# The gates of a gated-DeltaNet mixer as seven half-size products, with the combinations of x written over x

## The chip, the cores and the metric

The kernel runs on one core of a Trainium2 chip. The metric is the time of one execution on the device in microseconds (us); the median of three runs before the change is 1221.23 us (1221.22 to 1221.33). Beside the runs there is one profiled execution, whose trace the hardware profiler took. In what follows TensorE is the matrix engine (PE in the profile, PEld its loading of stationary operands), VectorE is DVE, ScalarE is ACT, GpSimd is POOL and SyncE is SP; a queue marked with a small q issues transfers.

## The reference, cut to what matters

A trunk of two layers over x of 512 tokens by 1024 channels, everything in float32. Layer 0 mixes tokens with gated linear attention (GLA), layer 1 with a gated DeltaNet (GDN); after each mixer comes a gated ConvFFN, and each sublayer ends in a LayerNorm of the scaled residual. The change lies in layer 1's mixer:

```python
def gdn_mixer(x, w_in, conv_w, a_log, dt_bias, norm_w, w_out):
    proj = x @ w_in
    qkv, gate, beta_lin, a_lin = ...            # gate: 512 x 1024
    ...
    o = rms_norm(gdn_chunked(qc, kc, vc, beta, gc), norm_w)
    return (from_head_chunks(o) * jax.nn.silu(gate)) @ w_out

def step(state, inp):                           # of gdn_chunked, over the chunks of tokens
    qk_n, u_n, w_n, qd_n, kd_n, cd_n = inp      # qd = q * exp(bcum)
    v_new = u_n - w_n @ state
    o_n = qd_n @ state + qk_n @ v_new
    state = state * cd_n + kd_n.T @ v_new
```

The gate is a product of x (512 x 1024) with 1024 columns of `w_in`. The kernel takes chunks of 128 tokens, four of them, for its eight heads.

## The kernel before, in words

**Numbers.** Each float32 operand of a large product is kept as a high part and a low part (`xh` and `xl`, `wh` and `wl`) in a type that TensorE takes in one pass, and a product is three matmuls: high with high, high with low, low with high. `split_out` (L715) makes the parts: a cast on ScalarE and a subtraction on VectorE, so both engines work on every weight tile. x itself lies in SBUF as `xh` and `xl`, eight chunks of 128 channels by 512 tokens, and is the operand of every projection of the mixer.

**Weights.** A plan lists all weight tiles in the order of their use. `issue` (L292) loads 128 x 1024 values into one of three buffers `raw` on SyncE's queue and splits them into one of four pairs `wh`, `wl`; `prefetch` runs two or three items ahead of the one taken.

**Order.** The kernel is traced by a planner with a clock of its own. `mm` (L208) adds the cost of each matmul to the clock. Generators (`spawn`) stand for the work beside the large products; each yields the clock time that it wants to let pass and is resumed by `pump` (L184), which is called after every few matmuls of a large product, or by `wait`, which lets the clock run on to the next generator that is due until a flag is set. Flags (`set`, `until`) are times of the planner, and what the chip waits for are the data dependences. A scheduler then places the instructions on the engines' queues by that order, and may take a later instruction where an earlier one isn't ready. Each engine works through its queue in order. Small tiles of 128 x 512 values come from 45 slots in this stage (`SLOTS`, L46).

**GLA's mixer** has its v and its gate as products in the form that the change brings to the other mixer: `plan_gated` (L282) plans the weights, `gated` (L1203) the products, and `x_forms` (L1149) makes the combinations of x, in eight pairs of extra slots. With x and the weight cut in two by two blocks, seven products of half the size in place of eight give the four blocks of the result; `GATED` lists them in order, weight combination and form of x: b21 with a12, b11 with a11, t1 with w1, b22 with v4, t2 with v2, t3 with v3, t4 with a22 (a11 and a12 are the even and odd chunks of tokens 0 to 255, a22 the odd chunks of the rest). The names in the profile are `fold` for their sums in PSUM, `xq` for the combinations and `xfh`, `xfl` for their parts. The weight combinations are made by transfers that add to what lies in SBUF (accumulating transfers, on GpSimd's queue) and by one addition on VectorE (L454).

**GDN's mixer** (`gdn`, L1590) runs the projections of k, v and q (`fm`), and beside them the inverses of small triangular matrices: in `base` on VectorE, with the 128 x 1024 tiles `tt` and `m2`, and in `inverses` on TensorE (`V`, `R`), in ten steps spread over the last projections and the first gate products. Step (half, 3) sets the flag ("rm", 5). Then `gates` (L1279) computes the gate in two halves of 512 columns through `x_tm` and `tm_half` (`tm<-wh,xh` and so on): per half eight channel chunks, four blocks of 128 tokens, three matmuls, each 128 x 128 by 512 columns, with a `pump` after every six. In between runs `chain` (L1888), one for each group of four heads, over four chunks of tokens. A turn of it: the state's product with k (`ks`) gives `yy` on VectorE (L1905); the inverse applied to it (`vn`) is scaled by ScalarE (L1913); k transposed (`kT`) is scaled by ScalarE (L1920); the state's product with q (`qs`) is scaled by VectorE (L1926); `s` updates the state on VectorE (L1936); `o` is added to the outputs on VectorE (L1944), whose squares ScalarE sums (L1946). `finish` (L1964) multiplies gate and output and transposes them (`yT`) for the output projection (`tm<-wh,yh`). After the gate, `unspill` brings the residual back and VectorE rescales it (L987, L988).

Of the kernel before, what the change touches and what calls it, by code (L numbers as in the profile page):

```python
# [8 lines left out]
F32 = mybir.dt.float32  # L9
# [6 lines left out]
P = 128  # L16
# [18 lines left out]
GATED_NEW = {"b21": "b21", "b11": "b11", "t1": "b12", "b22": "b22"}  # L35
GATED_IN = {"b21": "b21", "b11": "b11", "t1": "b11", "b22": "b22", "t2": "b11", "t3": "b22", "t4": "b11"}
GATED_SUM = {"t1": "b22", "b22": "b12", "t2": "b21"}
PREPARE = (4.0, 16.0, 48.0, 68.0)
PREPARE_APART = (2.0, 4.5)
LN_EPS = 1e-5  # L40
# [32 lines left out]
def blk(i, n=P):  # L73
    return slice(i * n, i * n + n)


class Trunk:
# [201 lines left out]
            for i in range(0, group["m"], 2):  # L279
                self.plan.append(("fold", group, name, quarter, i))  # L280

    def plan_gated(self, w, col):  # L282
        group = {"w": w, "col": col}
        for name, _, _ in GATED:
            for i in (0, 2):
                self.plan.append(("gated", group, name, i))
# [151 lines left out]
    def gated_load(self, group, name, i):  # L438


        if name not in GATED_NEW:
            return
        if name == "b11":
            t = self.mp.tile([P, 1024], F32, name=self.uid("gw"), tag="gw", bufs=2)
        else:
            t = self.rp.tile([P, 1024], F32, name=self.uid("raw"), tag="raw")
        self.nc.sync.dma_start(t.rearrange("p (j f) -> p j f", j=2), self.gated_rows(group, GATED_NEW[name], i))
        group[name, i] = t

    def issue_gated(self, group, name, i):  # L450
        nc = self.nc
        t = group[GATED_IN[name], i]
        if name == "t1":
            nc.vector.tensor_add(t, t, group.pop((name, i)))  # L454
            self.vec(1.24)
        self.held += 1
        wh = self.wp.tile([P, 1024], F32R, name=self.uid("wh"), tag="wh")
        wl = self.wp.tile([P, 1024], F32R, name=self.uid("wl"), tag="wl")
        self.split_out(wh, wl, t)
        self.vec(1.24)  # L460
        if name in GATED_SUM:
            nc.gpsimd.dma_start(t.rearrange("p (j f) -> p j f", j=2), self.gated_rows(group, GATED_SUM[name], i),
                                accum_op=ALU.add)
        if name in ("b21", "t3", "t4"):
            del group[GATED_IN[name], i]
        return [(wh[:, blk(j, S)], wl[:, blk(j, S)]) for j in range(2)]
# [101 lines left out]
    def tm_half(self, a, n, tail, done, slots=False, pieces=1):  # L568
# [19 lines left out]
        for tb in range(NTB):  # L588
            m = len(ps[tb])
            for piece in range(m):  # L590
# [5 lines left out]
                    done(tb, ps[tb][0])  # L596
                else:
                    done(tb, ps[tb][piece], piece, blk(piece, S // m))

    def x_tm(self, done):  # L600
        a = lambda c, tb: (self.xh[:, c, blk(tb)], self.xl[:, c, blk(tb)])
        self.tm_half(a, NC, 1, done)

    def out_proj(self, a, n, first, final, pieces=1):

# [543 lines left out]
    def x_forms(self, forms):  # L1149


        nc = self.nc
        pair = lambda t: t.rearrange("p (j i) -> p j i", j=2)

        def part(x, odd, tok, k):
            return x[:, 4 * k + odd:4 * k + odd + 3:2, tok:tok + 256]

        def full(odd, tok):
            ts = [self.slot("xq") for _ in range(2)]
            for k, t in enumerate(ts):  # L1160
                nc.vector.tensor_add(pair(t), *(part(x, odd, tok, k) for x in (self.xh, self.xl)))
            return ts

        def split(name, ts):
            forms[name] = []
            for t in ts:
                h, l = self.slot("xfh", F32R), self.slot("xfl", F32R)
                self.split_out(h, l, t)
                forms[name].append((h, l))
            self.set(("form", name), 2.0)  # L1170

        def both(a, b, op, out):
            for x, y, o in zip(a, b, out):
                nc.vector.tensor_tensor(o, x, y, op)

        for tb in range(NTB):
            yield from self.until(("x", tb))
        a = full(0, 256)
        yield 1.5
        b = full(1, 256)  # L1180
        yield 1.5
        both(a, b, ALU.subtract, b)
        yield 1.5
        split("w1", b)
        yield 2.0
        c = full(0, 0)
        yield 1.5
        both(c, a, ALU.subtract, a)
        yield 1.5
        both(b, c, ALU.subtract, b)  # L1190
        yield 1.5
        c = full(1, 0)
        yield 1.5
        both(b, c, ALU.add, c)
        yield 1.5
        split("v4", c)
        yield 2.0
        split("v2", b)
        b = c = None
        yield 2.0  # L1200
        split("v3", a)

    def gated(self, forms, tag, done, last):  # L1203


# [2 lines left out]
        top, high, right = ([None, None] for _ in range(3))  # L1208

        def operand(form, c, r):  # L1210
            if form in forms:
                cols = slice(c % 2 * 256 + r * P, c % 2 * 256 + r * P + P)
                return tuple(t[:, cols] for t in forms[form][c // 2])
            chunk = 2 * c + (form != "a11")
            tok = r * P + (256 if form == "a22" else 0)
            return self.xh[:, chunk, tok:tok + P], self.xl[:, chunk, tok:tok + P]
# [28 lines left out]
        for name, form, at in GATED:  # L1245
            if form[0] in "vw":
                self.wait(("form", form))
            def terms(i, w, r):
                for j in range(2):
                    begin = name in ("b11", "b21", "t1") and i + j == 0  # L1250
                    self.tm_terms(acc[at][r], *operand(form, i + j, r), *w[j], begin, i + j == 3, True)
                if i:
                    update(name, r)

            if name in ("t1", "t2", "t3"):
                w = [self.weight() for _ in range(2)]
                for r in range(2):
                    for i in (0, 2):
                        if name == "t3" and r and i:
                            self.look = 2  # L1260
                        terms(i, w[i // 2], r)
                        if name != "t3" or not r:
                            self.pump()
                        if r:
                            self.spend()
            else:
                for i in (0, 2):
                    w = self.weight()
                    if name == "t4":
                        self.after = ()  # L1270
                    for r in range(2):
                        terms(i, w, r)
                        self.pump()
                    self.spend()
            if last:
                forms.pop(form, None)
        self.look = LOOKAHEAD

    def gates(self, sg):  # L1279

        for hf in range(2):
            def done(tb, ps, hf=hf):
                t = self.slot("sg")
                self.nc.scalar.activation(t, ps, AF.Silu)
                sg[tb][hf] = t
                self.set(("sg", tb, hf), 2.0)

            self.x_tm(done)


    def gla_plan(self, w_in, w_out):
# [260 lines left out]
    def gdn_plan(self, w_in, w_out):  # L1552
        for hd in range(DH):
            if hd == HEADSTART:
                self.plan_pad([(w_in, 4096, 8, 0), (w_in, 4104, 8, H0)])
            self.plan_fm(w_in, 1024 + hd * P)
        for base in (2048, 0):
            for hd in range(DH):
                self.plan_fm(w_in, base + hd * P)
        for hf in range(2):  # L1560
            for cp in range(NC // 2):
                self.plan_tm(w_in, 2 * cp * P, 2, 3072 + hf * S)
        self.plan_out(w_out, 0, NC, TAIL)

    def gdn_consts(self, conv_w, a_log, dt_bias, norm_w):
# [24 lines left out]
    def gdn(self, li, g, b):  # L1590
# [297 lines left out]
        def chain(g):  # L1888
# [7 lines left out]
            for ck in range(4):  # L1896
# [24 lines left out]
                if ck > 0:  # L1921
                    ps = self.psum("qs")
                    for w, hd in heads:
                        self.mm(ps[:, w], q[hd][:, sl], s[:, w])
                    for w, hd in heads:
                        nc.vector.tensor_scalar_mul(vv[:, w], ps[:, w], eb[:, hd, one])  # L1926
                yield 1.4
                if ck < 3:
                    ps = self.psum("s")
# [31 lines left out]
                                           rr[:, hs4, :], ALU.mult, ALU.mult)  # L1961
            self.set(("r2", g), 2.5)

        def finish(hf):  # L1964
            for tb in range(NTB):
                yield from self.until(("sg", tb, hf))
            yield from self.until(("r2", hf))
            for tb in range(NTB):
                t = sg[tb][hf]
                for hd in range(4 * hf, 4 * hf + 4):  # L1970
                    w = blk(hd % 4)
                    last = nc.vector.scalar_tensor_tensor(t[:, w], v[hf][tb][:, w], r2[:, hd, tb:tb + 1], t[:, w],
                                                          ALU.mult, ALU.mult)
            yield 2.4
            self.split_y(y, hf, sg, self.gdn_nw, after=None if hf else last)

        items = [lambda ps, hd=hd: k_done(ps, hd) for hd in range(DH)]
        items.insert(HEADSTART, ba_done)
# [6 lines left out]
            self.spawn(chain(hg))  # L1985
        self.fm_items(items)
        for hf in range(2):
            self.spawn(finish(hf))
        self.gates(sg)
        self.wait(("r2", 1))  # L1990
        self.unspill(spilled)
        self.mixer_out(y, li, g, b)
# [76 lines left out]
```

## Time and profile before

| | us |
|---|---|
| median of three runs | 1221.23 |
| profiled execution, its own time | 1221.98 |
| its span, first to last instruction | 1220.2 |
| TensorE busy in the span | 1213.6 |
| VectorE busy | 906.1 |
| ScalarE busy | 609.4 |
| GpSimd busy | 160.7 |
| first to last matmul of GDN's gate (`tm<-wh,xh` and its kin, starts) | 724.6 to 813.0 |

The profiled execution took 1.78 us more than its span, and 0.75 us more than the median. Times inside the trace count from the first instruction. A group row gives line, engine, operation, written tile and read tiles, the count after x, then the busy time in us with the mean of one in ns, then the idle time of the engine just ahead of them with what ended it. A matmul row's duration contains its overlap with the next matmul; how fast matmuls follow each other is read from the chain of waits, which gives each piece its own time. A row "... x4" of the timeline gives the time from the first of four instructions to the end of the last.

### The profile page before, as it was taken

What the parts mean: (1) busy time and instruction counts of PE and PEld (TensorE: products, weight loads), DVE (VectorE), ACT (ScalarE), POOL (GpSimd) and SP (SyncE); (2) the same over time, 40 slices, a digit from 0 to 9 for tenths busy, and PEclk for the clock granted to TensorE, in tenths of its full rate; (3) what the DMA queues carried; (4) which work ended last, traced back from release to release, by engine and by line L of the source; (5) the groups of instructions that cost most, each with busy time, mean ns of one, the idle gap of its engine ahead of it and who ended that gap; (6) DMA issues with size and microseconds to landing.
All of it is one profiled execution on the core that took longest, in us unless ns stands there. A gap on an engine that the chain in (4) does not pass through costs nothing.

```text
span 1220.2 us, 17190 instructions
## 1 busy us (share of the span) xinstructions
PE 1213.6 (99%) x6501; PEld 1025.1 (84%) x6501; DVE 906.1 (74%) x1515; ACT 609.4 (50%) x1072; POOL 160.7 (13%) x203
## 2 busy tenths in 40 slices
PE   9999999999999999999999999999999999999998
PEld 8888888988888888889888888988988888888886
DVE  6989787787757675666789965688687757776667
ACT  5666663544434443454678555544644433443440
POOL 3030101601100110001242030200510100020000
PEclk9999999999999999999999999999999999999999
DMA  8384642536743554433444351335444853383311
GB/s 227 113 164 115 141 154 72 189 105 137 190 122 92 124 95 121 123 102 91 125 125 130 87 136 36 101 107 156 135 125 101 170 178 95 104 171 97 108 65 69
DMA packets 176275, 149.41 MB, mean 122 GB/s; under 512 B 16870, under 2 KB 140842, under 8 KB 176192
## 3 DMA queue, kind: packets, MB, share of 16 engines
q1 hardware_dynamic: 162464, 116.28, 32.2%
q0 software_dynamic: 12768, 31.37, 13.0%
q8 instruction: 51, 0.84, 0.3%
q10 hardware_dynamic: 960, 0.66, 0.2%
q14 instruction: 32, 0.26, 0.1%
HBM read 129.92 MB, written 5.78 MB: 111 GB/s over the span
## 4 chain that ended last, share of the span: by engine, by line
PE 97%; DMA 1%; ACT 1%; DVE 1%; SPq 0%; issue 0%; DVEq 0%
PE fm L213 54%; PE fold L213 19%; PE tm L213 15%; PE o L213 2%; PE xT L231 1%; DMA raw<-in_gla_w_in_dram 1%; PE pq L213 1%; PE pg L213 1%; PE vn L213 1%; PE yT L231 1%; PE V L213 0%; PE ds L213 0%; PE qs L213 0%; PE s L213 0%; PE ks L213 0%; DMA raw<-in_gdn_w_in_dram 0%
## 5 line engine op out<-in xcount | busy, mean ns | idle before, releaser
L213 PE MATMUL fm<-xh,wh 128*128 128x512 f32 (+2 forms) x1096 | 400.4, 368 | 0.7 <-ACT xh L716 0.7
L213 PE MATMUL fm<-xl,wh 128*128 128x512 f32 (+2 forms) x1096 | 398.5, 366 | 0.0
L213 PE MATMUL fm<-xh,wl 128*128 128x512 f32 (+1 forms) x1072 | 391.5, 367 | 0.2 <-DVE wl L716 0.2
L716 DVE TENSOR_TENSOR wl<-raw,wh 128x1024 fp32r<-128x1024 f32 (+1 forms) x158 | 195.4, 1239 | 151.7 <-ACT wh L716 151.3
L716 ACT CAST wh<-raw 128x1024 fp32r<-128x1024 f32 (+1 forms) x159 | 164.9, 1039 | 211.2 <-PE fm L213 135.5
L213 PEld LDWEIGHTS fm<-xh,wh 128*128 128x128 f32 (+1 forms) x1096 | 205.4, 188 | 34.1 <-ACT xh L716 0.9
L213 PEld LDWEIGHTS fm<-xl,wh 128*128 128x128 f32 (+1 forms) x1096 | 205.4, 188 | 32.6
L213 PEld LDWEIGHTS fm<-xh,wl 128*128 128x128 f32 x1072 | 201.2, 189 | 33.7 <-DVE wl L716 0.4
L1019 DVE SCALAR_TENSOR_TENSOR conv<-fm,ffn_cw,conv 128x511 f32<-128x511 f32 x112 | 83.5, 745 | 9.6 <-ACT conv L1017 7.9
L213 PE MATMUL fold<-wh,fh 128*128 128x512 f32 x224 | 87.6, 391 | 0.0
L213 PE MATMUL fold<-wh,fl 128*128 128x512 f32 x224 | 87.2, 389 | 0.0
L213 PE MATMUL fold<-wl,fh 128*128 128x512 f32 x224 | 87.1, 389 | 0.0
L716 ACT CAST wh<-b 128x1024 fp32r<-128x1024 f32 x48 | 50.0, 1054 | 74.2 <-PE fold L213 32.5
L716 DVE TENSOR_TENSOR wl<-b,wh 128x1024 fp32r<-128x1024 f32 x48 | 58.1, 1222 | 22.7 <-ACT wh L716 22.5
L412 POOL DMA_DIRECT2D b<-b x24 | 20.8, 902 | 357.2 <-DVE wl L716 306.7
L1037 ACT ACTIVATE conv<-conv 128x512 f32<-128x512 f32 x44 | 27.8, 632 | 63.3 <-DVE conv L1019 63.3
L1585 DVE SCALAR_TENSOR_TENSOR conv<-fm,gdn_cw,conv 128x511 f32<-128x511 f32 (+2 forms) x72 | 54.0, 788 | 5.1 <-ACT conv L1583 4.6
L213 PEld LDWEIGHTS fold<-wh,fh 128*128 128x128 f32 x224 | 42.0, 188 | 9.6 <-DVE h L1108 1.0
L213 PEld LDWEIGHTS fold<-wh,fl 128*128 128x128 f32 x224 | 42.0, 188 | 8.8
L213 PEld LDWEIGHTS fold<-wl,fh 128*128 128x128 f32 x224 | 42.1, 188 | 8.6
L1019 DVE SCALAR_TENSOR_TENSOR form<-fm,ffn_cw,form 128x511 f32<-128x511 f32 x64 | 47.7, 745 | 1.1
L929 POOL TENSOR_TENSOR h<-h,gb 128x512 f32<-128x512 f32 x16 | 24.1, 1525 | 135.5 <-PE xT L231 134.2
(363 smaller groups left out, 2009.1 us busy)
## 6 DMA issues: line engine op xcount, KB each, us to landing
raw<-in_ffn_w_in_dram SPq DMA_DIRECT2D x88, 512.0 KB, 3.9
raw<-in_gdn_w_in_dram SPq DMA_DIRECT2D x32, 512.0 KB, 4.1
b<-in_ffn_w_out_dram SPq DMA_DIRECT2D x24, 512.0 KB, 6.0
b<-b POOLq DMA_DIRECT2D x24, 512.0 KB, 4.8
raw<-in_ffn_w_out_dram SPq DMA_DIRECT2D x20, 512.0 KB, 3.7
raw<-in_gla_w_in_dram SPq DMA_DIRECT2D x18, 512.0 KB, 4.4
gw<-in_gla_w_in_dram POOLq DMA_DIRECT2D x8, 512.0 KB, 7.5
raw<-in_gla_w_out_dram SPq DMA_DIRECT2D x8, 512.0 KB, 3.7
```

The source lines that it names most:

```text
L213: t = self.nc.tensor.matmul(out, a, b, start=start, stop=stop, skip_group_check=joined)
L231: t = self.nc.tensor.transpose(out, a, self.ident[:n, :n])
L412: self.nc.gpsimd.dma_start(out, group[src, i][:, cols], accum_op=ALU.add)
L716: return self.nc.scalar.copy(dst_h, src), self.nc.vector.tensor_sub(dst_l, src, dst_h)
L929: nc.gpsimd.tensor_mul(h[hf], h[hf], gb[hf])
L1019: nc.vector.scalar_tensor_tensor(a[:, d:], ps[:, :S - d], tap(2 - d), a[:, d:], ALU.mult, ALU.add)
L1037: nc.scalar.activation(a, a, AF.Gelu)
L1585: self.conv = nc.vector.scalar_tensor_tensor(a[:, d:], ps[:, :S - d], tap(3 - d), a[:, d:], ALU.mult, ALU.add)
```

## The change

The gate of GDN's mixer becomes a `gated` product: seven products of four channel chunks (two of them to a weight item), two blocks of 128 tokens and three matmuls, and 14 weight items of two chunks instead of eight. The tiles of its first weight quarter (`b11`) take the places of `tt` and `m2`, and their sum with `b12` is now also made by an accumulating transfer. The combinations of x are made from ("rm", 5) on by the new `x_forms_within`, which needs at most six slots at a time, and their parts are written over those parts of `xh` and `xl` that no later product reads: w1 over the even chunks of tokens 256 to 511, v2 over the even chunks of tokens 0 to 255 once the product `b11` has read them, v4 over the odd chunks of tokens 0 to 255, v3 over w1 once that has been read. v4 is v2 plus the odd chunks, and this sum is made by four accumulating transfers inside SBUF. `finish` works on two token blocks at a time. In `chain`, ScalarE takes the scaling of `qs`. GLA's mixer keeps its path (`spare` false, `apart` true).

The diff, with the removal of `x_tm` and `gates` left out:

```diff
+SPARE = {0: "tt", 2: "m2"}
...
     def gated_load(self, group, name, i):
-        if name not in GATED_NEW:
+        spare = group["spare"]
+        if name not in GATED_NEW or (spare and name == "t1"):
             return
         if name == "b11":
-            t = self.mp.tile([P, 1024], F32, name=self.uid("gw"), tag="gw", bufs=2)
+            t = self.mp.tile([P, 1024], F32, name=self.uid("gw"), tag=SPARE[i] if spare else "gw", bufs=1 if spare else 2)
...
     def issue_gated(self, group, name, i):
-        if name == "t1":
+        if name == "t1" and not group["spare"]:
             nc.vector.tensor_add(t, t, group.pop((name, i)))
...
-        if name in GATED_SUM:
-            nc.gpsimd.dma_start(t.rearrange("p (j f) -> p j f", j=2), self.gated_rows(group, GATED_SUM[name], i),
+        added = "b12" if name == "b11" and group["spare"] else GATED_SUM.get(name)
+        if added:
+            nc.gpsimd.dma_start(t.rearrange("p (j f) -> p j f", j=2), self.gated_rows(group, added, i),
                                 accum_op=ALU.add)
...
+    def x_forms_within(self, forms, part, pair, full, both):
+        nc = self.nc
+        def put(name, ts, odd, tok):
+            for k, t in enumerate(ts):
+                self.split_out(part(self.xh, odd, tok, k), part(self.xl, odd, tok, k), pair(t))
+            forms[name] = (odd, tok)
+            self.set(("form", name), 2.0)
+        yield from self.until(("rm", 5))
+        a = full(0, 256)
+        yield 2.0
+        b = full(1, 256)
+        yield 2.0
+        both(a, b, ALU.subtract, b)
+        yield 2.0
+        put("w1", b, 0, 256)
+        yield 4.0
+        c = full(0, 0)
+        yield 2.0
+        both(c, a, ALU.subtract, a)
+        yield 2.0
+        both(b, c, ALU.subtract, b)
+        c = None
+        yield from self.until(("used", "a11"))
+        put("v2", b, 0, 0)
+        yield 2.0
+        for x in (self.xh, self.xl):
+            for k, t in enumerate(b):
+                nc.gpsimd.dma_start(pair(t), part(x, 1, 0, k).bitcast(F32), accum_op=ALU.add)
+        yield 9.0
+        put("v4", b, 1, 0)
+        b = None
+        yield from self.until(("used", "w1"))
+        put("v3", a, 0, 256)
...
     def gated(self, forms, tag, done, last):
         def operand(form, c, r):
+            if isinstance(forms.get(form), tuple):
+                odd, tok = forms[form]
+                chunk, tok = 2 * c + odd, tok + r * P
+                return self.xh[:, chunk, tok:tok + P], self.xl[:, chunk, tok:tok + P]
...
+            self.set(("used", form))
...
     def gdn_plan(self, w_in, w_out):
-        for hf in range(2):
-            for cp in range(NC // 2):
-                self.plan_tm(w_in, 2 * cp * P, 2, 3072 + hf * S)
+        self.plan_gated(w_in, 3072, True)
...
     def gdn(self, li, g, b):
-                        nc.vector.tensor_scalar_mul(vv[:, w], ps[:, w], eb[:, hd, one])
+                        nc.scalar.mul(vv[:, w], ps[:, w], eb[:, hd, one])
...
-        def finish(hf):
+        def finish(hf, half):
+            blocks = range(2 * half, 2 * half + 2)
...
+        def gate_done(tb, hf, t, src):
+            nc.scalar.activation(t, src, AF.Silu)
...
-            self.spawn(finish(hf))
-        self.gates(sg)
+            for half in range(2):
+                self.spawn(finish(hf, half))
+        forms = {"apart": False}
+        self.spawn(self.x_forms(forms))
+        self.gated(forms, "sg", gate_done, True)
```

More of the change, by code (lines that the diff above doesn't have):

```diff
@@ L280, in plan_fold, with plan_gated @@
                 self.plan.append(("fold", group, name, quarter, i))
-    def plan_gated(self, w, col):
-        group = {"w": w, "col": col}
+    def plan_gated(self, w, col, spare=False):
+        group = {"w": w, "col": col, "spare": spare}
         for name, _, _ in GATED:
@@ L598, in tm_half @@
                     done(tb, ps[tb][piece], piece, blk(piece, S // m))
-    def x_tm(self, done):
-        a = lambda c, tb: (self.xh[:, c, blk(tb)], self.xl[:, c, blk(tb)])
-        self.tm_half(a, NC, 1, done)
     def out_proj(self, a, n, first, final, pieces=1):
@@ L1174, in both @@
                 nc.vector.tensor_tensor(o, x, y, op)
+        if not forms.get("apart", True):
+            yield from self.x_forms_within(forms, part, pair, full, both)
+            return
         for tb in range(NTB):
@@ L1277, in gated @@
         self.look = LOOKAHEAD
-    def gates(self, sg):
-        for hf in range(2):
[L1282 to L1288, printed above, removed]
     def gla_plan(self, w_in, w_out):
@@ L1559, in gdn_plan @@
                 self.plan_fm(w_in, base + hd * P)
-        for hf in range(2):
-            for cp in range(NC // 2):
-                self.plan_tm(w_in, 2 * cp * P, 2, 3072 + hf * S)
+        self.plan_gated(w_in, 3072, True)
         self.plan_out(w_out, 0, NC, TAIL)
@@ L1962, in chain @@
             self.set(("r2", g), 2.5)
-        def finish(hf):
-            for tb in range(NTB):
+        def finish(hf, half):
+            blocks = range(2 * half, 2 * half + 2)
+            for tb in blocks:
                 yield from self.until(("sg", tb, hf))
             yield from self.until(("r2", hf))
-            for tb in range(NTB):
+            for tb in blocks:
                 t = sg[tb][hf]
@@ L1973, in finish @@
                                                           ALU.mult, ALU.mult)
-            yield 2.4
-            self.split_y(y, hf, sg, self.gdn_nw, after=None if hf else last)
+            yield 1.6
+            self.split_y(y, hf, sg, self.gdn_nw, blocks, last)
+        def gate_done(tb, hf, t, src):
+            nc.scalar.activation(t, src, AF.Silu)
+            sg[tb][hf] = t
+            self.set(("sg", tb, hf), 1.2)
         items = [lambda ps, hd=hd: k_done(ps, hd) for hd in range(DH)]
```

## The prediction

> **What bounds the kernel now.** I read the profile's page first: shares of busy time, then the granted clock by slices, then the chain that ended last.
>
> ```profile
> PE 1213.6 (99%) x6501; PEld 1025.1 (84%) x6501; DVE 906.1 (74%) x1515; ACT 609.4 (50%) x1072; POOL 160.7 (13%) x203
> ...
> PEclk9999999999999999999999999999999999999999
> ...
> PE 97%; DMA 1%; ACT 1%; DVE 1%; SPq 0%; issue 0%; DVEq 0%
> ```
>
> TensorE is busy 99% of the span at the full granted clock, and 97% of the chain is TensorE. Only fewer matmuls, or less waiting that the change itself brings, can move the time. So the second view is the busy time of each engine by stage. The first two rows are GLA's two gated products, the others GDN's gate up to its second product, the stretch in which the chunk loop runs beside it, and the output projection behind the gate.
>
> ```profile
> 59.00:111.00 52.00, 52.00 (x275) 43.48 (x274) 47.31 (x79) 35.68 (x63) 11.07 (x13) 1.00 0.69 155
> 111.00:163.00 52.00, 51.93 (x287) 43.34 (x286) 42.17 (x105) 35.97 (x67) 7.09 (x6) 1.00 0.47 102
> ...
> 724.40:748.80 24.40, 24.38 (x344) 20.27 (x343) 15.00 (x41) 12.06 (x42) 0.00 (x0) 1.00 0.25 80
> 748.80:770.40 21.60, 21.60 (x169) 20.55 (x169) 12.68 (x36) 13.23 (x50) 0.00 (x0) 1.00 0.11 29
> ...
> 813.00:850.00 37.00, 37.00 (x171) 30.49 (x169) 33.93 (x61) 14.91 (x21) 0.00 (x0) 1.00 0.49 145
> ```
>
> Columns are the stage's length, then busy us of PE, PEld, DVE, ACT and POOL. TensorE never pauses here. GLA's rows show that the same seven-product form runs without a gap, with VectorE at 47.31 of 52.00, but there the forms of x are ready long before. In GDN's gate VectorE has 8.9 us free of 21.6 in the second stretch, ScalarE 8.4.
>
> The third view is the chain in order of time, which here is TensorE's own order: start, length, piece.
>
> ```profile
> 742.75 1.59 PE tm L213 x6
> ...
> 747.20 1.58 PE tm L213 x6
> 748.78 0.89 PE ks L213 x8
> ...
> 751.00 1.39 PE tm L213 x6
> ...
> 770.38 1.40 PE tm L213 x6
> ...
> 791.88 0.89 PE o L213 x8
> ...
> 799.31 19.66 PE tm L213 x86
> ```
>
> Six gate matmuls, then pieces of the chunk loop, in turn. The gate's matmuls by stage:
>
> ```profile
> 724.40:748.80 24.40, 13.07 (x48) 8.49 (x48) 0.00 (x0) 0.00 (x0) 1.00 0.25 80
> 748.80:770.40 21.60, 6.82 (x25) 4.51 (x26) 0.00 (x0) 0.00 (x0) 1.00 0.11 29
> ```
>
> By 748.8 48 are done, and four more packs of six by 770.38. In the new form these are exactly two products (b21, b11) and then the third (t1). So, in the order of before, form w1 is due at 748.8 to 751.0 and form v4 at 770.4.
>
> **The change part by part.**
>
> *Matmuls, the gain.* Before: 2 halves x 8 chunks x 4 blocks x 3 = 192. After: 7 x 4 chunks x 2 blocks x 3 = 168, of the same shape. Where they run undisturbed, 86 take 19.66 us, 0.229 us each; 24 fewer give -5.5 us. All of it is on the path, since TensorE has no gap in the stage.
>
> *Added work.* Its prices come from these groups, GLA's forms among them:
>
> ```profile
> L716 ACT CAST wh<-raw 128x1024 fp32r<-128x1024 f32 (+1 forms) x159 | 164.9, 1039 | 211.2 <-PE fm L213 135.5 <-PE fold L213 37.5 <-PE tm L213 14.8
> L716 DVE TENSOR_TENSOR wl<-raw,wh 128x1024 fp32r<-128x1024 f32 (+1 forms) x158 | 195.4, 1239 | 151.7 <-ACT wh L716 151.3
> L1174 DVE TENSOR_TENSOR xq<-xq,xq 128x512 f32<-128x512 f32 x8 | 5.2, 684 | 0.1
> L716 ACT CAST xfh<-xq 128x512 fp32r<-128x512 f32 x8 | 4.8, 616 | 2.8 <-DVE xq L1174 2.8
> L716 DVE TENSOR_TENSOR xfl<-xq,xfh 128x512 fp32r<-128x512 f32 x8 | 5.4, 684 | 0.1
> 754.38 1.16 ACT L1920 ACTIVATE kd<-kT,gd_ebl 128x128 f32<-128x128 f32 x4
> 754.65 1.13 DVE L1926 TENSOR_SCALAR v<-qs,gd_eb 128x128 f32<-128x128 f32 x4 [2.69 <-PE qs L213]
> L412 POOL DMA_DIRECT2D b<-b x24 | 20.8, 902 | 357.2 <-DVE wl L716 306.7 <-DMA b<-b 43.6 <-DVE h L1106 6.8
> b<-b POOLq DMA_DIRECT2D x24, 512.0 KB, 4.8
> gw<-in_gla_w_in_dram POOLq DMA_DIRECT2D x8, 512.0 KB, 7.5
> ```
>
> VectorE: 12 sums and differences and 8 low parts, 20 x 0.684 = 13.7 us; 6 more weight tiles x 1.24 = 7.4; 4 block updates x 0.68 = 2.7; away go 6 scalings of four, 6 x 1.13 = 6.8. Net +17 us in the gate's 83 (724.6 to 813.0, less 5.5). ScalarE: 8 x 0.616 = 4.9; 6 x 1.04 = 6.2; 6 copies of sums at the price of such a cast, 3.7; 6 x 1.16 = 7.0 for the moved scaling, at the price of the like scaling of `kT`. Net +22 us. As sums both fit; what matters is the stretch before v4 is due.
>
> *Form w1.* Step (half, 3) is the piece of TensorE ahead of the pack at 742.75; six VectorE operations take 4.1 us, and in the row 724.40:748.80 VectorE has 9.4 us free. From the pump behind that pack, at 744.3, the sums are ready at 748.4, a cast and a subtraction later the first half at 749.7, the second at 750.4. From 748.8 to the pack at 751.0 TensorE has pieces of the loop, 2.2 us. Cost 0, at most 2.5 us if every VectorE operation has to queue once.
>
> *Form v4, the loss.* After w1 come the third sum and two differences, 6 x 0.684 = 4.1 us on a VectorE about half busy, so some 8 us: 758.5. The split of v2 takes 2.1, with queueing: 761. Then four accumulating transfers, two rounds, since the low part adds to the same tile as the high part: one issue of 0.9 us and twice the landing of `b<-b`, 4.8 us (twice the bytes of one of these, but the nearest row): 10.5, so 771.5. The split of v4 takes 2.1: 773.6. It is due at 770.4, 3.2 us before that. In those TensorE still has pieces of the chunk loop, but ScalarE, which paces them, is short just then: in 748.80:770.40 it has 13.23 us of work, and there come 3 x 1.16 for `qs`, 4 x 0.616 for the halves of w1 and v2, one more weight cast 1.04, two Silus like casts, 2 x 0.62: 21.5 of 21.6 us. So I count two thirds of the 3.2 us as lost: +2.0. Bounds: 0, if the steps are placed earlier than the planner asks for, since VectorE has room before 748.8; +8, if each step waits for a pump and the loop falters as well.
>
> The Trainium skill ("DMA: Bandwidth & Descriptors", Anatomy of one DMA) puts a transfer from GpSimd's queue at 2.0 us plus its bytes at 436 GB/s, by which a 256 KB round would take 2.6 us, as an estimate. By that, v4 would come 4.4 us sooner, ahead of its due time, and the loss would be nothing. For 512 KB the same rule gives 3.2 us where the row of `b<-b` has 4.8, so the trace speaks for the longer time.
>
> *Weights.* Four quarters loaded and eight accumulating transfers, on queues that were empty (POOL 0.00 in 724.40:770.40). The shortest turn is b11's, two items ahead of t1: 12 matmuls an item, two items at least 5.5 us and here with the loop's pieces over 10, against 7.5 us for `gw`, and the items run three ahead. Cost 0; without that lead the 2 us between 7.5 and 5.5.
>
> *The moved scaling.* It takes 1.13 us of each turn from VectorE and puts 1.16 on ScalarE, between the scaling of `kd` and the squares, with the addition of `o` behind it. The loop's last `o` ended at 792.8 in before and the gate at 813, so a few us of delay there are hidden; the cover is the gate's remaining 96 matmuls (22 us) behind v4. In the stretch before v4 its cost is in the +2.0.
>
> *The end.* VectorE was at 33.93 of 37.00 behind the gate with TensorE never waiting; some of its new work slips into that stage, which starts 5.5 us earlier. GLA's rows show the like without a gap. I take +0.4, bounds 0 and 3.
>
> Sum: -5.5 + 0 + 2.0 + 0 + 0.4 = -3.1 us. On the profiled execution's 1221.98 (its span of 1220.2 and 1.78 around it) that is 1218.9; that execution stood 0.75 above the median of 1221.23, so the median should be 1218.1.
>
> **The rivals.**
>
> *The gain is eaten (no change).* Each step of the forms waits for a pump, and pumps lie 4 to 5 us apart (four packs of six from 751.00 to ahead of 770.38). Then the third sum falls at about 757, the differences at 762, v2's split at 766 to 768.5, the transfers end at 779, v4 at 781: 10.6 us late. Two turns of the loop are left for that time, and they are paced by ScalarE; with a third of it lost, +3.6. -5.5 + 3.6 + 0.4 = -1.5: 1219.7. For it: ScalarE's 21.5 of 21.6. Also here belongs the shortage of slots: 32 for q, v, the decays and the inverses, 2 states, 2 for the first sums, 6 for forms leave 3 of 45 for the loop's six. Against: the scheduler may take a ready step early.
>
> *The transfers hold ScalarE's queue (slower).* The cast of v4 is put into ScalarE's queue where the landing is expected. This view of the tile `b` gives the spread:
>
> ```profile
> DMA to landing us min/median/max: 3.6/5.6/9.8
> ...
> ACT wh L716 <- DMA b<-b: 17.5, 8, 4.2
> ```
>
> ScalarE did wait for such transfers, 17.5 us in 8 times, 4.2 at worst. At 9.8 us a round instead of 4.8 the cast waits 10 us longer, behind it wait the scalings of `vn` and `kd`, and with them the loop and then TensorE: -5.5 + 2.0 + 10 + 0.4 = +6.9, 1228.1. It decides from a wait of some 5.5 us beyond the forecast. Against: in GDN's stretch the transfer engines are busy 0.11 to 0.25 of the time, and the loop can use what ScalarE did before.
>
> The Trainium skill ("SBUF — State Buffer", SBUF: two separate sides) warns that a two-port VectorE operation keeps GpSimd from writing descriptors, which would make those landings late. In GLA's stage, with VectorE at 47.31 of 52.00, the transfers into `gw` landed within 7.5 us in the median, so no row here shows it.
>
> *The whole gain.* v4 in time, nothing lost: 1221.23 - 5.5 = 1215.7.
>
> That the matmuls don't go away isn't possible; the count is in the code.
>
> **How the numbers follow.** A measurement of this kernel can tell about 0.2% (2.4 us) from no change. The forecast with losses up to 3 us, 0.33; the whole gain, 0.19; both are faster: 0.52. Gain eaten, losses of 3 to 8 us: 0.30. Transfers or slots holding up the loop, beyond that: 0.18, slower. The range, 1215.6 to 1223.5, holds the first three cases but their edges and leaves out some 0.17, nearly all above; the forecast's own range is 1215.6 to 1218.8.
>
> **What would show it.** In the new trace: 168 matmuls of `fold` in GDN's gate and none of `tm<-wh,xh`; TensorE's busy time lower by 5.5 us; idle time of TensorE or of its loading, ended by a cast or subtraction of `xh`, `xl` at form v4 (about 2 us), none or little at w1; the second pair of transfers landing 10 us behind v2's split; ScalarE near full between 749 and 771; the output projection free of gaps. The prediction is wrong if TensorE waits anywhere else in the loop, if ScalarE waits for a transfer with the loop behind it, or if idle time stands in the output projection.

## The result and the profile after

The changed kernel took 1232.24 us in the median of four runs (1231.64 to 1232.70), the kernel before beside it 1221.28: ratio 1.0089 (1.0072 to 1.0107), 11 us slower where 3.1 us faster was forecast, and outside the predicted range. The profiled execution took 1232.38 us, its span 1230.5, 10.3 more than before.

The page's busy times, and the chain that ended last:

```profile
PE 1213.1 (99%) x6477; PEld 1023.8 (83%) x6477; DVE 925.2 (75%) x1523; ACT 629.1 (51%) x1116; POOL 174.8 (14%) x215
...
PE 95%; DVE 2%; DMA 1%; issue 1%; POOL 0%; ACT 0%; SPq 0%; DVEq 0%; ACTq 0%; POOLq 0%
```

The 24 matmuls are gone (6501 to 6477), but TensorE is only 0.5 us less busy, and its idle time grew from 6.6 us (1220.2 - 1213.6) to 17.4. So there are two losses, waits and slower matmuls. The busy times by stage (length, PE, PEld, DVE, ACT, POOL, then granted clock, share of the transfer engines, GB/s) show both between 724 and 813:

```profile
724.40:748.80 24.40, 22.94 (x334) 18.83 (x332) 18.63 (x44) 14.29 (x39) 6.00 (x5) 1.00 0.77 137
748.80:770.40 21.60, 21.60 (x176) 20.70 (x174) 17.52 (x40) 19.15 (x80) 1.19 (x1) 1.00 0.25 38
770.40:793.00 22.60, 18.52 (x137) 17.15 (x135) 15.54 (x40) 17.20 (x62) 14.00 (x18) 0.96 0.77 161
793.00:813.00 20.00, 16.28 (x67) 13.15 (x66) 16.37 (x49) 8.90 (x18) 0.00 (x0) 0.87 0.46 135
...
785.00:790.00 5.00, 2.13 (x15) 1.50 (x13) 2.00 (x4) 0.75 (x3) 5.00 (x8) 1.00 1.18 206
790.00:795.00 5.00, 3.79 (x14) 3.42 (x15) 2.85 (x12) 3.57 (x15) 1.51 (x3) 0.66 0.97 235
805.00:810.00 5.00, 2.15 (x6) 1.73 (x7) 4.90 (x11) 2.70 (x5) 0.00 (x0) 0.82 0.01 3
```

In the kernel before, TensorE was busy without a pause in the last two of these stages, at the full clock:

```profile
770.40:793.00 22.60, 22.60 (x163) 20.89 (x163) 15.25 (x56) 12.34 (x53) 6.42 (x12) 1.00 0.40 131
793.00:813.00 20.00, 20.00 (x99) 16.76 (x98) 15.21 (x49) 8.67 (x18) 0.00 (x0) 1.00 0.44 134
```

ScalarE at 19.15 of 21.60 is nearly as full as forecast (21.5), and TensorE waits for nothing there. The waits lie elsewhere (who waits, for what, us in all, times, longest):

```profile
PE fold L214 <- DVE sg L1279: 3.7, 1, 3.7
PE fold L214 <- ACT xh L715: 2.5, 1, 2.5
PE xT L232 <- DVE h L891: 1.6, 1, 1.6
PE o L214 <- ACT vn L1945: 1.6, 1, 1.6
PE vn L214 <- DVE rm L1869: 1.5, 1, 1.5
```

The timeline around the first two (start, us, piece, and in brackets the wait ahead of it):

```profile
765.07 0.69 DVE L1160 TENSOR_TENSOR xq<-xh,xl 128x512 f32<-128x512 f32 x1 [2.03 <-PE vn L214]
768.93 0.69 DVE L1160 TENSOR_TENSOR xq<-xh,xl 128x512 f32<-128x512 f32 x1
775.63 1.28 DVE L715 TENSOR_TENSOR xl<-xq,xh 128x512 fp32r<-128x512 f32 x2
777.81 2.46 POOL L1236 DMA_DIRECT2D xq<-xh  x2 [1.48 <-DVE xl L715]
783.14 1.19 POOL L1236 DMA_DIRECT2D xq<-xl  x1 [1.65 <-DMA xq<-xh]
784.59 1.18 POOL L1236 DMA_DIRECT2D xq<-xl  x1 [0.27 <-DMA xq<-xh]
788.25 0.62 ACT L715 CAST xh<-xq 128x512 fp32r<-128x512 f32 x1 [3.11 <-DMA xq<-xl]
788.92 0.50 PE L214 MATMUL fold<-wh,xh 128*128 128x512 f32 x1 [2.52 <-ACT xh L715]
790.27 0.62 ACT L715 CAST xh<-xq 128x512 fp32r<-128x512 f32 x1 [1.41 <-DMA xq<-xl]
790.80 1.13 ACT L1945 ACTIVATE vn<-vn,gd_bp 128x128 f32<-128x128 f32 x4
791.21 2.08 PE L214 MATMUL o<-vn,dt 128*128 128x128 f32 x8 [1.56 <-ACT vn L1945]
801.93 1.05 ACT L715 CAST wh<-gw 128x1024 fp32r<-128x1024 f32 x1 [1.89 <-PE fold L214]
805.40 1.07 ACT L1264 COPY sg<-fold 128x512 f32<-128x512 f32 x2
807.12 1.27 DVE L1279 TENSOR_TENSOR sg<-sg,fold 128x512 f32<-128x512 f32 x2
807.85 0.50 PE L214 MATMUL fold<-wh,xh 128*128 128x512 f32 x1 [3.72 <-DVE sg L1279]
```

Read it downward. The two tiles of `c` come 4 us apart, the first when a `vn` matmul has let go of a slot; v2's split ends at 776.9 (775.63 + 1.28); GpSimd issues the high parts' transfers, then, as each lands, the low parts'; ScalarE stands at v4's two casts until 788.25 and 790.27, with the scaling of `vn` behind them. TensorE waits 2.52 us for v4 and 1.56 for `vn`. In the third wait, t3 must not write its sum before t2's is subtracted; the subtraction needs b22's sum copied by ScalarE, and that copy stands in its queue behind weight casts that wait for buffers (the last two start at 801.93 and 803.30) and behind two scalings of `yT`. Behind these waits the matmuls themselves are slow: eight `o` took 2.08 us (0.89 before), and the clock is 0.66 and 0.82.

### The profile page after: what moved, and what is told of

It reads as the page before. It is cut to its first block, busy times and chain, and to the rows that moved or that the text cites. A ratio compares the mean times of both kernels' runs of the same rounds, so it can differ in the third digit from the quotient of the medians.

```text
span 1230.5 us, 17237 instructions
## 1 busy us (share of the span) xinstructions
PE 1213.1 (99%) x6477; PEld 1023.8 (83%) x6477; DVE 925.2 (75%) x1523; ACT 629.1 (51%) x1116; POOL 174.8 (14%) x215
## 4 chain that ended last, share of the span: by engine, by line
PE 95%; DVE 2%; DMA 1%; issue 1%; POOL 0%; ACT 0%; SPq 0%; DVEq 0%; ACTq 0%; POOLq 0%
PE fm L214 53%; PE fold L214 21%; PE tm L214 13%; PE o L214 2%; PE xT L232 1%; PE pg L214 1%; DVE wl L715 1%; DMA gw<-in_gdn_w_in_dram 1%; PE yT L232 0%; DMA xq<-xl 0%; PE V L214 0%; PE ds L214 0%; PE vn L214 0%; PE s L214 0%; PE ks L214 0%
## 5 line engine op out<-in xcount | busy, mean ns | idle before, releaser
L214 PE MATMUL fold<-wh,xh 128*128 128x512 f32 x104 | 43.9, 422 | 6.3 <-DVE sg L1279 3.7
```

Of the source, the lines that this page charges most:

```text
L214: t = self.nc.tensor.matmul(out, a, b, start=start, stop=stop, skip_group_check=joined)
```

## The experiments

Two theories were set against each other first. A: the accumulating transfers, with in-order queues behind them, take the time. B: ScalarE, given the scaling, holds up the loop. C, the shortage of slots, came third. Times are medians; "before" ran beside each group at 1221.07, 1221.19 and 1221.30.

**One part alone: the scaling on ScalarE, in the kernel before.**

```diff
-                        nc.vector.tensor_scalar_mul(vv[:, w], ps[:, w], eb[:, hd, one])
+                        nc.scalar.mul(vv[:, w], ps[:, w], eb[:, hd, one])
```

> The kernel before with one part of the change alone: ScalarE scales `qs`. Theory A (the transfers into the forms and weights, with in-order queues behind them, take the time; the moved scaling is harmless): within 2 us of before, 1219.5 to 1223; TensorE idle in the loop not above before's. Theory B (ScalarE, with 7 us more work in the loop, holds the loop up): 1225 or more, with TensorE waiting for `vn` or for `o`'s addition in 750 to 795.

1221.34, ratio 1.0001 (0.9992 to 1.0011), no wait of TensorE in the loop. B falls.

**The scaling back on VectorE, in the changed kernel.** The same line the other way.

> The changed kernel with the scaling of `qs` back on VectorE. Theory A: 1230 to 1234, the stalls at forms v4 and at t3 stay (VectorE has 1.1 us more in each turn, so the forms come a little later still). Theory B: some 4 us of the 11 come back, 1226 to 1228, and the wait of `o` for `vn` (1.6 us) goes.

1235.74, ratio 1.0119 (1.0104 to 1.0134): worse by 3.5 us, above what either theory said. The moved scaling is a help beside the forms, not a cost.

**v4 by VectorE.**

```diff
-        for x in (self.xh, self.xl):
-            for k, t in enumerate(b):
-                nc.gpsimd.dma_start(pair(t), part(x, 1, 0, k).bitcast(F32), accum_op=ALU.add)
-        yield 9.0
-        put("v4", b, 1, 0)
+        c = full(1, 0)
+        yield 2.0
+        both(b, c, ALU.add, c)
+        yield 2.0
+        put("v4", c, 1, 0)
```

> The changed kernel with v4 made by four VectorE operations (odd chunks summed in two more slots, then added to v2) in place of four accumulating transfers. Theory A (transfers): v4 is ready some 3 to 4 us behind v2's split, at about 782 to 784, before TensorE asks for it; the waits of 2.5 and 1.6 us at 786 to 791 and the fall of the clock behind them go: 1232.2 - 4.1 - 2 = 1226 (1224.5 to 1228). Theory C (slots: the forms come late because 45 slots are too few): the two further slots come late as well, a wait of 2 us or more stays at v4: 1229 to 1233.

1221.12, ratio 1.0000 (0.9990 to 1.0009): all 11.1 us come back, 5 more than the 1226 expected. The waits of this version and its busy times:

```profile
PE vn L214 <- DVE rm L1869: 1.5, 1, 1.5
...
PE xT L232 <- DVE h L891: 0.9, 1, 0.9
...
PE fold L214 <- DVE sg L1279: 0.2, 1, 0.2
...
PE 1209.4 (99%) x6477; PEld 1020.2 (84%) x6477; DVE 925.1 (76%) x1527; ACT 628.7 (52%) x1116; POOL 172.5 (14%) x211
```

With the same 6477 matmuls TensorE is busy 3.7 us less than in the changed kernel: that is the price of the slower clock. Idle time is 9.5 us (1218.9 - 1209.4) instead of 17.4, 7.9 less. The two make the 11.6 by which the spans differ. The wait at t3 went too, though nothing was changed there: the first copy of b22's sum now stands right behind its matmuls in ScalarE's order, at 790.89.

**Two more slots.** `SLOTS = 47` in the changed kernel.

> The changed kernel with 47 slots in this stage instead of 45. Theory C (slots): the second tile of `c` is made right behind the first (765.8 instead of 768.9), the differences and v2's split come 3 us sooner or more, so the transfers land by 786 and the wait at v4 goes; the copy of b22's sum too if it waited for a slot: 1223 to 1227. Theory A (transfers): the landing stays two rounds of 5.3 us behind the split and the casts stay in front of the `vn` scaling: 1229 to 1233.

1229.04, ratio 1.0061 (1.0044 to 1.0078). The second tile of `c` came right behind the first, as C said, and 3.2 us came back: the waits of `o` and of `xT`, 1.6 us each, are gone from the list. But v2's split, which also waits for the loop's turn on both engines, ended no sooner (777.8), and the waits at v4 and t3 stayed at 2.5 and 3.5 us. Slots are a part of it, not the cause.

**The sum of b11 and b12 by VectorE,** as in the other mixer: t1 loads b12 into a `raw` buffer and adds it.

> The changed kernel with the sum of b11 and b12 made as in the other mixer: b12 loaded into a `raw` buffer and added by VectorE, instead of the accumulating transfer. If the wait of 1.5 us at 742 (`vn` for the copies `rm`, which stand on VectorE behind a weight tile whose transfer landed late) comes from that transfer's landing, it goes: 1232.2 - 1.5 = 1230.7 (1229.5 to 1231.5), and the stalls at v4 and t3 stay. If the wait comes from the inverses' own chain, it stays: 1232 to 1233.5, VectorE having 2 x 1.24 us more.

1231.28, ratio 1.0079 (1.0064 to 1.0094). Its waits:

```profile
PE fold L214 <- ACT xh L715: 4.0, 1, 4.0
PE fold L214 <- DVE sg L1279: 3.7, 1, 3.7
PE xT L232 <- DVE h L891: 1.4, 1, 1.4
...
PE o L214 <- ACT vn L1945: 0.4, 1, 0.4
```

The 1.5 us at `vn` are gone, so the late transfer had made them (ScalarE's cast of `gw` had waited 2.42 us for it at 739.19, VectorE's subtraction for the cast, and the copies `rm` stood behind that). The wait at v4 is longer, 4.0 instead of 2.5, but the one for `vn` behind it shorter, 0.4 instead of 1.6: together 4.4 for 4.1, so little was given back there. TensorE and v2's split both came to that place 1.7 us sooner, yet v4's transfers landed no sooner, since their rounds took 5.2 to 7.6 us here instead of 5.0 to 5.7. Why they took longer is open.

**Both sums by VectorE.**

> v4 and the sum of b11 and b12 both by VectorE. The version with v4 alone took 1221.1 with 1.5 us of waiting at 742 left. If the transfers are all that stood against the gain: 1219.6 (1218.8 to 1220.4). If VectorE becomes the bound (it has about 2.5 us more before 750): 1221 or more, with TensorE waiting for VectorE in the loop.

1219.33, ratio 0.9985 (0.9975 to 0.9994), as expected from the transfers alone: the other 1.8 us show once v4 is no longer made by transfers.

**The forms sooner, with their transfers:** the pauses of 2 and 4 us that the planner is told to leave between the steps of the forms cut to 0.2.

> The changed kernel with its transfers, but with the planner's pauses of 2 and 4 us between the steps of the forms cut to 0.2 us (the 9 us ahead of v4's split stay), so that both tiles of `c` and v2's split stand earlier in the queues. If v4 is late because its inputs are late (slots and pauses), v2's split is done 3 us sooner or more, the transfers land by 786, the wait at v4 goes: 1225 to 1228. If the two rounds of transfers are late whenever they start (each 5.3 us, with ScalarE's casts in front of the `vn` scaling), the stalls stay: 1230 to 1233.

1226.06, ratio 1.0040 (1.0025 to 1.0055). v2's split ended at 770.7, 6 us sooner, and v4 was in time for b22; 6.2 us came back. But now ScalarE's queue holds the loop:

```profile
780.83 0.62 ACT L715 CAST xh<-xq 128x512 fp32r<-128x512 f32 x1 [5.33 <-DMA xq<-xl]
781.35 1.13 ACT L1945 ACTIVATE vn<-vn,gd_bp 128x128 f32<-128x128 f32 x4
...
PE qs L214 <- ACT vn L1945: 3.2, 1, 3.2
```

**v4's casts behind the loop's scaling,** on top of the last: the planner waits for the seventh scaling of `vn`, and the casts are ordered behind it.

```diff
-        yield 9.0
-        put("v4", b, 1, 0)
+        while len(self.turns) < 7:
+            yield 0.4
+        for k, t in enumerate(b):
+            cast, _ = self.split_out(part(self.xh, 1, 0, k), part(self.xl, 1, 0, k), pair(t))
+            self.behind(cast, self.turns[6])
```

> The changed kernel with its transfers and the shorter pauses (1226.1), and v4's casts put behind the seventh scaling of `vn` in ScalarE's queue, so that the sixth and seventh, 5.3 us behind the waiting cast before, no longer wait for the landing. If the in-order queue is what turns the landing into TensorE's wait, the 3.2 us of `qs` for `vn` go, and some of the clock's fall: 1221.5 to 1223.5. If v4 itself is late for b22, the wait moves to `fold` behind the casts: 1225 to 1227.

1221.21, ratio 1.0004 (0.9995 to 1.0014), a little under the forecast, but less steady than before: three of the ten runs took 1223.4 to 1224.8. The same transfers, landing at the same times, now cost nothing in the median, measured against v4 by VectorE (1221.12):

```profile
775.84 1.14 ACT L1951 ACTIVATE vn<-vn,gd_bp 128x128 f32<-128x128 f32 x4 [0.28 <-PE vn L214]
779.84 1.25 ACT L1951 ACTIVATE vn<-vn,gd_bp 128x128 f32<-128x128 f32 x4
781.85 0.78 ACT L715 CAST xh<-xq 128x512 fp32r<-128x512 f32 x1
782.88 0.62 ACT L715 CAST xh<-xq 128x512 fp32r<-128x512 f32 x1 [0.24 <-DMA xq<-xl]
```

The scaling that had waited until 781.35 starts at 775.84, and the cast waits 0.24 us. The edit also moved the copies of b22's sum forward (t3's wait fell from 1.3 to 0.3 us), so about a microsecond of the 4.9 is theirs.

**The residual's loads behind v4's transfers** in GpSimd's queue, in the changed kernel.

> The changed kernel with the residual's eight loads (`h` from `hd`) put behind v4's four accumulating transfers in GpSimd's queue. If those loads, 2 MB beside the accumulating transfers, lengthen the rounds (5.0 to 5.7 us) or hold the queue, v4 comes 1 to 2 us sooner: 1230 to 1231.5. If the rounds take their 5 us anyway and start when v2's split is done (778.7): 1231.7 to 1233.

1232.24, ratio 1.0086 (1.0071 to 1.0101): no difference in the median. (The 778.7 in the expectation is the end of a later subtraction; v2's own split ended at 776.9.) The profile doesn't say that the loads are harmless, though. The casts of v4 start 10.4 and 11.8 us behind the end of v2's split, against 11.3 and 13.4 in the changed kernel, and TensorE's waits for v4 and `vn` are 1.6 and 0.9 us instead of 2.5 and 1.6. What this saves is hidden by 2.0 us more of busy time (1215.1 for 1213.1); the clock fell behind an earlier wait, which the last section shows. The four runs spread from 1229.57 to 1233.44. So the loads may cost 1 to 2 us; they are not the cause of the 11.

**Both sums by VectorE and 47 slots.**

> v4 and the sum of b11 and b12 by VectorE, with 47 slots. If slots still delay the forms in that version, 0.5 to 1.5 us better than the same with 45: 1218 to 1219.5. If they don't matter once no transfer stands between v2 and v4: the same as with 45, within 0.5 us.

1218.77, ratio 0.9980 (0.9970 to 0.9989): faster than both kernels. Against 45 slots the 0.56 us are within the two intervals, so whether the slots still matter stays open. The profiles hint that they do: TensorE's wait of 1.3 us at `xT`, in the version with 45 slots, is gone, as it went in the changed kernel with two more slots.

**The same with the scaling back on VectorE.**

> The version with v4 and the sum of b11 and b12 by VectorE and 47 slots (1218.8), with the scaling of `qs` back on VectorE. The moved scaling alone was worth nothing in the kernel before (0.0 us), and taking it back cost the changed kernel 3.5 us. If its worth is the room on VectorE that the forms need: 1219.5 to 1222 here, with TensorE waiting for VectorE in 770 to 813. If those 3.5 us were only the transfers' stalls made longer: 1218.3 to 1219.3.

1233.03, ratio 1.0092 (1.0075 to 1.0109): 14 us worse, which neither side expected. The timeline of this version, then the one row of the version with the scaling on ScalarE that answers to its second:

```profile
793.20 1.22 DVE L715 TENSOR_TENSOR wl<-gw,wh 128x1024 fp32r<-128x1024 f32 x1
794.97 1.22 POOL L465 DMA_DIRECT2D gw<-in_gdn_w_in_dram  x1 [8.56 <-ACT sg L1264]
803.76 1.04 ACT L715 CAST wh<-gw 128x1024 fp32r<-128x1024 f32 x1 [7.27 <-DMA gw<-in_gdn_w_in_dram]
804.84 1.23 DVE L715 TENSOR_TENSOR wl<-gw,wh 128x1024 fp32r<-128x1024 f32 x1 [5.60 <-ACT wh L715]
807.46 0.68 DVE L1282 TENSOR_TENSOR sg<-sg,fold 128x512 f32<-128x512 f32 x1
808.28 0.76 PE L214 MATMUL fold<-wh,xh 128*128 128x512 f32 x1 [7.29 <-DVE rs_t L734]
```

```profile
787.79 1.22 POOL L465 DMA_DIRECT2D gw<-in_gdn_w_in_dram  x1 [2.56 <-ACT xh L715]
```

A transfer that adds to `gw` can start only when VectorE has split what lies there. With four more VectorE operations in each turn, that split ended at 794.4, the transfer went out 7.2 us later than with ScalarE's help, took 8.7 us to land, and TensorE stood 7.3 us; the clock of 793 to 813 was 0.83. (The row of the transfer names ScalarE's copy as its releaser, but in both versions it goes out some 0.55 us behind the end of that split.) The landing itself did not end TensorE's wait. TensorE adds t4 to the sum that holds t3, so VectorE must first subtract that sum as it stands (L1282), and in VectorE's queue this subtraction stood behind the split of the late tile, from 804.84 on; it ran at 807.46. So here too an accumulating transfer took the time, this time of the weights that both versions kept, and again through what stood behind its consumer in a queue. This reading rests on the one profile; the four runs (1231.8 to 1233.7) agree in time.

**The best version with the shorter pauses.**

> The same version (1218.8, scaling on ScalarE) with the planner's pauses between the steps of the forms cut to 0.2 us. No wait at the forms is left in it, so if the forms are early enough: the same, 1218.3 to 1219.3. If VectorE's queue is so tight that forms made sooner delay the loop: 1219.5 or more.

1220.36, ratio 0.9992 (0.9983 to 1.0001): 1.6 us worse, and not by a wait in the loop but by 1.6 us of `fm` for `xl` (L912), where the sublayer behind begins. How an earlier form leads to that is open.

## Why the prediction was wrong, step by step

**Matmuls (-5.5): nearly right.** From each matmul's start to the next one's, summed over the timeline, 192 gate matmuls held TensorE 46.32 us before, and 168 hold it 41.26 in the best version (v4 and the weights' sum by VectorE, 47 slots): -5.06. There 1.1 us are given back by the small matmuls of the inverses (8.7 to 9.8 us, 0.56 of it a wait for a transfer of `T`) and 0.5 by `o`. Its median is 2.4 below before, its profiled span 3.2.

**Added work (VectorE +17, ScalarE +22): about right.** Busy time rose by 19.1 us (925.2 - 906.1) and by 19.7 (629.1 - 609.4). On VectorE the prediction counted four block updates, where the code makes six (two each at L1272, L1279 and L1282), 1.4 us more.

**Form w1 (0): right in cost, wrong in time.** Its split ended at 762.0, not 750.4, yet TensorE had pieces of the loop to do in place of the gate's, as the row of 748.80 to 770.40 shows.

**Form v4 (+2.0, bounds 0 to 8): this step failed.** The lateness was about right, since both sides slipped: v2's split at 776.9 for 761, the landings 11.3 and 13.3 us behind it (788.2 and 790.2) for 10.5, b22 due at 786.4 for 770.4, so 2.5 us late for 3.2. What it cost was not: "two thirds" of the lateness became 11.1 us, above the upper bound. It was 2.5 us for v4, 1.6 for the `vn` scaling behind its second cast, 3.5 at t3, 3.7 of slower matmuls, and 0.7 of the wait of `xT` (12.0 together; the spans differ by 11.6, and these are the differences to the version with v4 by VectorE). For the 3.5 at t3 no run moves the copies of b22's sum alone, so why they were placed so late in ScalarE's order along with the transfers stays open. The sum priced a late form by its lateness alone; neither the place of casts and copies in ScalarE's queue, nor the clock behind a wait, had a term. The rival of the transfers that hold ScalarE's queue named the mechanism, with 1228.1, and the run with the casts moved shows it; given 0.18 together with slots, it was held too small, on the ground that the transfer engines were idle. But it had another reason for the wait, rounds of 9.8 us, and there it was wrong: the rounds took 5.0 to 5.7 us, near the 4.8 of the nearest row. Rounds not much longer than forecast were enough, since v2 was late and the casts stood ahead of the scaling of `vn`.

The Trainium skill ("DMA: Bandwidth & Descriptors", Anatomy of one DMA) would give a round of 256 KB 2.6 us, as an estimate. The changed kernel measured 5.0 to 5.7, and all runs that kept these transfers 3.7 to 7.6, so the measurement decides, as the prediction had it.

**Weights (0; 2 without the lead): wrong.** b11's second transfer was issued at 732.44, landed after 6.7 us, and its cast had stood 2.4 us: TensorE lost 1.5, within the 2 that the prediction gave for the case without the lead. The prediction took the lead of two items for granted and did not follow VectorE's queue, where the copies `rm`, which `vn` needs, stood behind the waiting weight tile.

**The moved scaling (0): right alone** (0.0), but beside the forms it is worth 3.5 us and, in the best version, 14. The prediction counted it as a load on ScalarE and put it into v4's loss; it is what keeps VectorE's splits, and with them the weight transfers, on time.

**The end (+0.4, bounds 0 to 3): within bounds.** `xT` waits 1.6 us for VectorE in the changed kernel, and not at all in the best version.

Of the signs that the prediction set for itself, 168 matmuls of `fold`, no wait at w1, some 2 us idle at v4 (2.5), transfers landing some 10 us behind v2's split and ScalarE near full came true; TensorE busy 5.5 us less and an output projection without gaps did not, and the waits elsewhere in the loop, which it had named as the sign that it is wrong, are there.

## What to carry to other kernels

A transfer in the middle of a chain is priced by what stands behind its consumer in an in-order queue, not by its landing alone: the same four transfers cost 11 us, 5 once v2 came 6 us sooner, and nothing in the median once the casts also stood behind the loop's scaling. Where an engine waits for a landing, list what is queued behind that instruction and put it ahead, or do the sum on an engine that has room (11 us here for four VectorE operations; with the weights' sum done so too the change gains 0.15%, with two more slots 0.2%). Add to the waits of the bound engine what its clock may lose behind them: 3.7 us here for two falls.

## What was not expected of the hardware

The granted clock falls behind short waits. After the 3.72 us at t3 the matmuls follow each other every 0.43 us, from 808.55 to 811.5, instead of every 0.23. It fell even behind a wait of 1.60 us; this is the stretch around the `vn` wait at 742 in the run with the residual's loads moved:

```profile
740.00:742.50 2.50, 1.09 (x7) 0.79 (x5) 1.60 (x3) 2.45 (x3) 0.11 (x1) 1.00 0.86 153
742.50:745.00 2.50, 2.30 (x28) 2.00 (x30) 1.88 (x6) 1.31 (x7) 1.41 (x2) 0.82 0.45 32
745.00:747.50 2.50, 2.50 (x22) 2.09 (x19) 0.75 (x2) 1.47 (x5) 0.86 (x1) 0.50 0.91 146
747.50:750.00 2.50, 2.50 (x20) 2.25 (x19) 1.51 (x3) 0.63 (x1) 0.00 (x0) 1.00 1.06 188
```

At the same place the wait of 1.46 us in the changed kernel left the clock at 1.00, and so did the one of 1.56 us in the run with the forms sooner. So the length of the wait hardly decides alone; what else does, no run here shows. The Trainium skill ("TensorE: Matmul & The Clock Gate", Part 1: The HAM clock gate) says that the clock is halved when a window of some 3.4 us was idle and comes back after about as long a busy one. The half rate and the 3 to 4 us until it ends agree with the rows above; that a wait of 1.6 us was once enough differs from it, and the measurement decides.
